# Half products of 21 `up` pairs on an x2 that is not yet normalised

## The chip, the core and the metric

One core of a Trainium2 chip runs the whole kernel, one hybrid decoder layer on 512 tokens of width 1024. The metric is the device time of one execution in microseconds (us). The time before is the median of 3 runs.

Engines are named as the profile names them: PE is TensorE (matmuls; PEld its weight loads), DVE is VectorE, ACT is ScalarE, POOL is GpSimd, SP is SyncE. SP issues the plain DMAs, GpSimd those that add to what lies at their destination (`accum_op`, here called accumulates).

## The reference

Only the last part of the layer is changed. `x` after the attention part is called x2 in the kernel.

```python
def rms_norm(x, g):
    xf = x.astype(jnp.float32)
    y = xf * lax.rsqrt(jnp.mean(xf * xf, axis=-1, keepdims=True) + RMS_EPS)
    return (y * g.astype(jnp.float32)).astype(x.dtype)
...
        x = x + (gate_pool * y_pool + gate_nsa * y_nsa) @ w_out[l]
        h = rms_norm(x, ffn_norm_g[l])
        gate_pre, val = jnp.split(h @ w_up[l], 2, axis=-1)
        gate_c = causal_dwconv(gate_pre, conv_w[l], conv_b[l])
        x = x + (jax.nn.silu(gate_c) * val) @ w_down[l]
```

`D_MODEL` is 1024, `D_FF` 2816, `CONV_WIDTH` 3 and `DEPTH` 1. The norm's factor is one number per token; the gain `g` is one number per feature.

## The kernel before

**Layout and precision.** Activations lie transposed: 128 features on the partitions, 512 tokens along the free axis, so x2 is 8 tiles of 128 x 512. Each float32 operand a of a product is split into a high part and a low part in the matmul's rounded float32 type, and a product is three matmuls: high by high, high by low, low by high. `split` makes the high part on ACT and the low one on DVE; `split_by_dma` writes -x on ACT into the low tile, rounds x into the high tile on ACT, and has a GpSimd DMA add x to the low tile. Weights are loaded as raw tiles of 128 x 1024 into rings of three (`wraw`, and `whi`, `wlo` for their parts).

**Order.** No instruction is issued where the code stands. `Plan` records every operation with what it reads and writes, then plays the whole list through with its own costs, gives each operation a due time, and writes out an order for each engine (line 395 issues all of them, so every row of the profile has line 395). TensorE keeps the order of recording (in the attention part it merges two such streams); DVE, ACT, POOL and SP are ordered by due time. The engines run these orders strictly; semaphores do the rest. Small working tiles come from a pool of 54 pages of 128 x 512.

**Stages.** After the attention part come the products with `w_nsa_out` (lines 1081 to 1102), then `out` (lines 1107 to 1124): for f in 0, 4, 1, 5, 2, 6, 3, 7, 24 matmuls of 512 columns give one tile of x2; it is added to x, multiplied by the gain and split into gh and gl, and its square goes into `acc`. `norm_rstd` (line 556) sums `acc` over the features by 8 small matmuls and takes the inverse root on DVE in twelve small steps; `bcast_rstd` (line 565) spreads the result over the partitions as `rb` by way of four diagonal tiles and 8 matmuls.

**`up`, `w_up` in 22 pairs.** Pair f is 128 columns of gate_pre and the same 128 of val. `up_plain` (line 1173), for f = 0 to 3, multiplies gh, gl by both weight tiles, 24 matmuls of 512 columns each, and multiplies by `rb` behind PSUM. In pair 0 the norm's matmul stands behind the gate's 24 matmuls, and the broadcast behind the first 15 of val's.

`up_fast` (line 1260), for f = 4 to 21, sees a pair as a 2 x 2 product of halves: the features in two halves of 4 tiles, the tokens in two halves of 256 columns, the two weight tiles as the other side. With seven half products instead of eight (and sums of halves on either side) it gets the same four results. A half product (`product`, line 1199) is 4 x 3 matmuls of 256 columns. The sums of the weights' halves (`s3`, `h1` to `h5`) are made on DVE from the raw halves `rg`, `r1`, `r2`, and four of the five are split with an accumulate. The loads of r1 and r2 wait for the first product of the pair two before (`begun[-2]`, line 1263). The sums of x2's halves are made once, in `halves` (line 1140), on x2 already multiplied by the gain and by `rb`; that is why it stands behind pair 0. It gives nh and nl (x2's halves themselves) and th and tl (their sums).

Three PSUM banks serve a pair: bx, by and bq. The first product goes to bx and is copied to by, on which the second goes on; two results on the way are read off by ACT (u2 and u3, the halves of `u1`) and added by DVE to what bq holds. Two of the seven products are put off into the next pair (`held`: `end1`, `end2`), and with them the pair's `conv` (a bias and three taps, then Silu) and the split of y = silu x val.

**`down`.** y's first 16 tiles go into x2 in four groups of four, each group 8 products of 12 matmuls of 512 columns, called fills here (`dn_group`, line 1227). `AT` says before which pair a group is ready, and `FILL` how many fills stand where: one number ahead of the pair, and three inside it. The first group starts with `both`, which takes two banks. y's last 6 tiles are multiplied at the very end (lines 1341 to 1360).

**The start.** Eight matmuls of a tile of ones (line 495) run while the first loads are under way.

Of the kernel before, what the change touches and what calls it, by code (L numbers as in the profile page):

```python
# [15 lines left out]
P = 128  # L16
# [3 lines left out]
KD = 8  # L20
# [32 lines left out]
PLAIN = 4  # L53
DIRECT = (0, 3)
AT = (4, 9, 13, 17)
FILL = {f: (0, 0, 0, 0) for f in range(22)}
FILL.update({4: (0, 4, 0, 0), 5: (0, 1, 0, 0), 6: (0, 1, 0, 0), 7: (0, 1, 0, 0), 8: (0, 1, 0, 0)})
FILL.update({f: (0, 1, 1, 0) for f in range(9, 18)})
# [340 lines left out]
def hybrid_layer(ctx: ExitStack, tc: tile.TileContext, xT, pos, par, cst, poolw, w1, wa, wb, wf,  # L399
# [95 lines left out]
    for i in range(8):  # L495
        PE.matmul(pt[:, 0:P], ones, ones, start=(i == 0), stop=(i == 7))
# [59 lines left out]
    def norm_rstd(acc_tile, dst, tag):  # L556
        pt = bank(tag)
# [19 lines left out]
    for k in range(KD):  # L577
# [6 lines left out]
        if k == 6:  # L584
            for j in range(KD):
                square_x(j)
            norm_rstd(acc, rstd, "mm")
            DVE.tensor_scalar_mul(rhalf, rstd, 0.5)
# [515 lines left out]
    x2, gh, gl = [None] * KD, [None] * KD, [None] * KD  # L1104
    acc = page("acc")
    ffng = R("ffng")
    for f in (0, 4, 1, 5, 2, 6, 3, 7):
# [6 lines left out]
        tail = pl.last()  # L1114
        x2[f] = pl.tile(sb, (P, T), F32, "x2", "pp", 10)
        DVE.tensor_add(x2[f], pt, xres)
        gh[f], gl[f] = page("gh", dt=F32R), page("gl", dt=F32R)
        split(gh[f], gl[f], x2[f], ffng[:, f:f + 1])
        if f:
            sq = page("sq")  # L1120
            ACT.activation(sq, x2[f], AF.Square)
            DVE.tensor_add(acc, acc, sq)
        else:
            ACT.activation(acc, x2[f], AF.Square)

    rstd2 = keep("rstd", (P, NT))
    convb = R("convb")
    nh, nl, th, tl = {}, {}, {}, {}
    yh, yl = [None] * KF, [None] * KF
    tt = pl.tile(sb, (P, 4, T), F32R, "th", "ptc", 1)  # L1130
    t2 = pl.tile(sb, (P, 3, T), F32R, "th", "t_cst", 1)
    t3 = [pl.tile(sb, (P, T), F32R, n, "t_" + n, 1) for n in ("oraw", "ot")]
    b11 = [[pl.tile(sb, (P, T), F32R, "nh", "pt", 6) for _ in range(2)] for _ in range(2)]

    def split_by_dma(hi, lo, x):
        ACT.activation(lo, x, AF.Copy, scale=-1.0)
        POOL.dma_start(lo, x, accum_op=ALU.add)
        ACT.activation(hi, x, AF.Copy)

    def halves(k):  # L1140
        u = [page("xb"), page("xb")]
        for x, j in zip(u, (k, k + 4)):
            DVE.scalar_tensor_tensor(x, x2[j], ffng[:, j:j + 1], rb, op0=ALU.mult, op1=ALU.mult)
        c = slice((k % 2) * H2, (k % 2 + 1) * H2)
        nh[k], nl[k] = (b11[k // 2][i][:, c] for i in range(2))
        split(nh[k], nl[k], u[0][:, :H2])
        nh[k + 4] = pl.tile(sb, (P, T), F32R, "nh", "pt", 6) if k < 2 else page("nh", dt=F32R)
        nl[k + 4] = pl.tile(sb, (P, T), F32R, "nl", "pp", 10) if k < 2 else page("nl", dt=F32R)
        split_by_dma(nh[k + 4], nl[k + 4], u[1])
        b1, b2 = u[0], u[1]  # L1150
        ta, tb = page("ta"), page("tb")
        DVE.tensor_sub(ta[:, :H2], b1[:, :H2], b1[:, H2:])
        DVE.scalar_tensor_tensor(ta[:, H2:], ta[:, :H2], -1.0, b2[:, H2:], op0=ALU.mult, op1=ALU.subtract)
        DVE.tensor_sub(tb[:, :H2], b2[:, H2:], b1[:, H2:])
        DVE.scalar_tensor_tensor(tb[:, H2:], ta[:, H2:], -1.0, b2[:, :H2], op0=ALU.mult, op1=ALU.subtract)
        for i, x in ((0, ta), (1, tb)):
            th[k, i] = tt[:, k] if i == 0 else t2[:, k] if k < 3 else t3[0]
            tl[k, i] = page("tl", dt=F32R) if k or i else t3[1]
            (split_by_dma if i else split)(th[k, i], tl[k, i], x)

# [12 lines left out]
    def up_plain(f):  # L1173
        pts = []
        for s in range(2):
# [9 lines left out]
            if f == 0 and s == 0:  # L1185
                norm_rstd(acc, rstd2, "tr")
# [269 lines left out]
```

## Time and profile before

| | |
|---|---|
| median of 3 runs | 693.01 us (692.36 to 693.43) |
| the profiled execution | 693.21 us |
| its span, first to last instruction | 691.4 us |
| matmul records | 4060 |
| DMA packets | 45703, 113.99 MB |

How to read the rows that follow: a group's row gives engine, operation, the tiles written and read by the program's names (buffer numbers left out), the shape, the number of instructions, then their busy time and the mean ns of one, then the engine's idle time before them and what ended it. The wait view names who was waited for, the time in all, how often, and the longest. The chain of waits follows the work that ended last back to the start, and is listed in order of time: start, length, what. The timeline lists start and length of each instruction. Spans of matmuls overlap, since they are pipelined; the spacing of two starts is what one costs.

### The profile page before, as it was taken

Reading aid. Unit: us, or ns where it says so; the run is one execution under the profiler, and the core shown is the slowest. Engines: PE = TensorE matmul, PEld = TensorE weight load, DVE = VectorE, ACT = ScalarE, POOL = GpSimd, SP = SyncE. Lnnn points to the kernel's source line nnn. Section 1 sums busy time; section 2 is a strip of 40 time slices with the busy share of each in tenths; the row PEclk is TensorE's granted clock in tenths of the full one; section 3 lists DMA queues with packets and bytes.
Section 4 is the critical chain, followed back from the end, with each engine's and each line's share of the span. In section 5 each row is a group of like instructions: output and inputs, shape, how many; then the busy total and the mean of one; then the engine's idle time right before and its main releaser. Section 6 shows DMA issues by size and latency. Waiting matters only on the chain.

```text
span 691.4 us, 11144 instructions
## 1 busy us (share of the span) xinstructions
PE 687.2 (99%) x4060; PEld 606.8 (88%) x4060; DVE 479.6 (69%) x1032; ACT 432.2 (63%) x795; POOL 98.3 (14%) x124
## 2 busy tenths in 40 slices
PE   9999999999999999999999999999999999999998
PEld 8898978888888888888888899999999999999987
DVE  6768568878787644765569967777776766675542
ACT  7667677776777653334459758778677656674320
POOL 0011100000000000000022223223222112220000
PEclk9999999999999999999999999999999999999999
DMA  8468534655556557844379778779888866764131
GB/s 299 143 164 248 139 105 92 155 137 138 152 122 151 154 137 229 278 152 144 125 159 255 173 176 210 171 168 225 203 198 189 205 155 159 179 168 101 46 129 62
DMA packets 45703, 113.99 MB, mean 165 GB/s; under 512 B 5328, under 2 KB 6096, under 8 KB 45648
## 3 DMA queue, kind: packets, MB, share of 16 engines
q1 hardware_dynamic: 29520, 76.43, 34.3%
q0 software_dynamic: 15840, 36.71, 29.5%
q8 instruction: 32, 0.52, 0.3%
q14 instruction: 23, 0.19, 0.1%
q10 hardware_dynamic: 288, 0.14, 0.1%
HBM read 70.27 MB, written 6.29 MB: 111 GB/s over the span
## 4 chain that ended last, share of the span: by engine, by line
PE 99%; DMA 0%; ACT 0%; DVE 0%; SPq 0%; issue 0%; ACTq 0%
PE mm L395 42%; PE tr L395 32%; PE sc L395 14%; PE av L395 11%; DMA xr<-xT 0%; ACT xh L395 0%; DVE o L395 0%; SPq L395 0%; ACTq L395 0%
## 5 line engine op out<-in xcount | busy, mean ns | idle before, releaser
L395 ACT ACTIVATE whi<-wraw 128x1024 fp32r<-128x1024 f32 (+2 forms) x96 | 97.1, 1013 | 70.4 <-issue 29.0
L395 DVE TENSOR_TENSOR wlo<-wraw,whi 128x1024 fp32r<-128x1024 f32 (+1 forms) x66 | 76.3, 1158 | 15.6 <-ACT whi L395 14.6
L395 POOL DMA_DIRECT2D wlo<-wraw x30 | 25.9, 865 | 331.6 <-ACT wlo L395 273.9
L395 PE MATMUL mm<-xh,whi 128*128 128x512 f32 x176 | 73.0, 415 | 0.0
L395 PE MATMUL mm<-xh,wlo 128*128 128x512 f32 x176 | 69.1, 393 | 0.0
L395 PE MATMUL mm<-xl,whi 128*128 128x512 f32 x176 | 68.9, 391 | 0.0
L395 PE MATMUL mm<-tl,sh 128*128 128x256 f32 x190 | 53.5, 282 | 0.0
L395 PE MATMUL mm<-th,sl 128*128 128x256 f32 x174 | 49.1, 282 | 0.0
L395 PE MATMUL mm<-th,sh 128*128 128x256 f32 x174 | 49.0, 281 | 0.0
L395 ACT ACTIVATE wlo<-wraw 128x1024 fp32r<-128x1024 f32 x30 | 31.7, 1060 | 21.6 <-PE mm L395 13.6
L395 POOL DMA_DIRECT2D sl<-r x36 | 31.0, 860 | 87.0 <-ACT sl L395 64.6
L395 PE MATMUL sc<-yh,whi 128*128 128x512 f32 x104 | 40.5, 389 | 0.0
L395 PE MATMUL sc<-yl,whi 128*128 128x512 f32 x104 | 40.5, 389 | 0.0
L395 PE MATMUL sc<-yh,wlo 128*128 128x512 f32 x104 | 40.5, 389 | 0.0
L395 PEld LDWEIGHTS mm<-xh,wlo 128*128 128x128 f32 x176 | 33.0, 188 | 7.5
L395 DVE SCALAR_TENSOR_TENSOR ft<-fg,pr,ft 128x511 f32<-128x511 f32 (+1 forms) x44 | 32.9, 749 | 9.6 <-ACT ft L395 8.9
L395 ACT ACTIVATE pp<-pp,asm 128x384 f32<-128x384 f32 (+3 forms) x64 | 35.4, 557 | 5.8 <-DVE asm L395 5.8
L395 PEld LDWEIGHTS mm<-xh,whi 128*128 128x128 f32 x176 | 33.2, 188 | 4.6
L395 PEld LDWEIGHTS mm<-xl,whi 128*128 128x128 f32 x176 | 33.3, 189 | 4.2
L395 PEld LDWEIGHTS mm<-tl,sh 128*128 128x128 f32 x190 | 35.7, 188 | 0.4
L395 PEld LDWEIGHTS mm<-th,sh 128*128 128x128 f32 x174 | 32.7, 188 | 1.0
L395 PEld LDWEIGHTS mm<-th,sl 128*128 128x128 f32 x174 | 32.7, 188 | 0.0
(399 smaller groups left out, 2078.9 us busy)
## 6 DMA issues: line engine op xcount, KB each, us to landing
wlo<-wraw POOLq DMA_DIRECT2D x30, 512.0 KB, 4.5
wraw<-wup SPq DMA_DIRECT2D x26, 512.0 KB, 4.0
wraw<-wf SPq DMA_DIRECT2D x22, 512.0 KB, 3.6
r<-wup SPq DMA_DIRECT2D x36, 256.0 KB, 5.0
sl<-r POOLq DMA_DIRECT2D x36, 256.0 KB, 5.4
wraw<-wdn SPq DMA_DIRECT2D x16, 512.0 KB, 4.1
sl<-s POOLq DMA_DIRECT2D x18, 256.0 KB, 5.9
sl<-wraw POOLq DMA_DIRECT2D x18, 256.0 KB, 4.7
```

The costliest lines, as they stand in the source:

```text
L395: getattr(self.real[o.eng], method)(*a, **kw)
```

## The change

- `PLAIN` is now (0,): pairs 1, 2 and 3 are taken by `up_fast` too, so 21 of 22 pairs use half products. `AT` begins at 5 instead of 4, and pairs 1 to 4 have no fill; pairs 5 to 17 have two each, 18 to 21 one each. `both` is gone.
- The sums of x2's halves are made by `sums(k)` inside `out`, as soon as x2[k] and x2[k + 4] are there, on x2 times the gain. `halves`, nh and nl are gone; gh and gl take their places, and are kept for all pairs.
- What comes out of PSUM in `up_fast` is multiplied by `rb`: two copies become multiplications by `rb` on DVE (one of the two was on ACT), and two sums get a multiplication behind them.
- The third product of the first pair by half products, which has none put off from before it, stands second.
- r1 and r2 of pairs 1 and 2 wait for groups of `out`, since `begun` now begins with these.
- The norm's matmul takes another PSUM bank, and nine matmuls of ones run at the start instead of eight.

```diff
 NCST = _o
 PAGES = 54
 RINGS = {"wraw": 3, "whi": 3, "wlo": 3}
-PLAIN = 4
-DIRECT = (0, 3)
-AT = (4, 9, 13, 17)
+PLAIN = (0,)
+DIRECT = (0,)
+AT = (5, 9, 13, 17)
 FILL = {f: (0, 0, 0, 0) for f in range(22)}
-FILL.update({4: (0, 4, 0, 0), 5: (0, 1, 0, 0), 6: (0, 1, 0, 0), 7: (0, 1, 0, 0), 8: (0, 1, 0, 0)})
-FILL.update({f: (0, 1, 1, 0) for f in range(9, 18)})
+FILL.update({f: (0, 1, 1, 0) for f in range(5, 18)})
 FILL.update({18: (0, 1, 0, 0), 19: (0, 1, 0, 0), 20: (0, 1, 0, 0), 21: (0, 1, 0, 0)})
 TRIES = 12
 RESERVE = 3
...
     POOL.memset(ones, 1.0)
     ACT.dma_start(pr[:, 0:16], par[:, 0:16])
     pt = bank("mm")
-    for i in range(8):
-        PE.matmul(pt[:, 0:P], ones, ones, start=(i == 0), stop=(i == 7))
+    for i in range(9):
+        PE.matmul(pt[:, 0:P], ones, ones, start=(i == 0), stop=(i == 8))
     xr, xh, xl = [None] * KD, [None] * KD, [None] * KD
     acc = page("acc")
...
     rb = keep("rb", (P, T))
-    def norm_rstd(acc_tile, dst, tag):
-        pt = bank(tag)
+    def norm_rstd(acc_tile, dst, pt):
         with pl.unit():
             for t in range(NT):
                 PE.matmul(pt[:, t:t + 1], acc_tile[:, t * P:(t + 1) * P], ones[:, 0:1], start=True, stop=True)
...
             if f > 1:
                 tail = nots[f - 2]
-    x2, gh, gl = [None] * KD, [None] * KD, [None] * KD
+    x2, gh, gl, begun = [None] * KD, [None] * KD, [None] * KD, []
     acc = page("acc")
     ffng = R("ffng")
+    less = keep("less", (P, KD))
+    DVE.tensor_scalar_mul(less, ffng, -1.0)
+    th, tl = {}, {}
+    tt = pl.tile(sb, (P, 4, T), F32R, "th", "ptc", 1)
+    t2 = pl.tile(sb, (P, 3, T), F32R, "th", "t_cst", 1)
+    t3 = [pl.tile(sb, (P, T), F32R, n, "t_" + n, 1) for n in ("oraw", "ot")]
+
+    def split_by_dma(hi, lo, x):
+        ACT.activation(lo, x, AF.Copy, scale=-1.0)
+        POOL.dma_start(lo, x, accum_op=ALU.add)
+        ACT.activation(hi, x, AF.Copy)
+
+    def sums(k):
+        a, b = x2[k], x2[k + 4]
+        ta, tb, b2 = page("ta"), page("tb"), page("b2")[:, :H2]
+        ACT.activation(b2, b[:, H2:], AF.Copy, scale=ffng[:, k + 4:k + 5])
+        DVE.tensor_sub(tb[:, H2:], a[:, :H2], a[:, H2:])
+        ACT.activation(ta[:, :H2], tb[:, H2:], AF.Copy, scale=ffng[:, k:k + 1])
+        DVE.scalar_tensor_tensor(tb[:, :H2], a[:, H2:], less[:, k:k + 1], b2, op0=ALU.mult, op1=ALU.add)
+        DVE.scalar_tensor_tensor(ta[:, H2:], ta[:, :H2], -1.0, b2, op0=ALU.mult, op1=ALU.subtract)
+        DVE.scalar_tensor_tensor(tb[:, H2:], b[:, :H2], less[:, k + 4:k + 5], ta[:, H2:], op0=ALU.mult, op1=ALU.subtract)
+        for i, x in ((0, ta), (1, tb)):
+            th[k, i] = tt[:, k] if i == 0 else t2[:, k] if k < 3 else t3[0]
+            tl[k, i] = page("tl", dt=F32R) if k or i else t3[1]
+            (split_by_dma if i else split)(th[k, i], tl[k, i], x)
+
     for f in (0, 4, 1, 5, 2, 6, 3, 7):
         xres = page("xres")
         with pl.behind(tail):
...
         pt = any_bank()
         mm3(pt, wh, wl, mh, ml, 0, KD)
         tail = pl.last()
+        begun.append(tail)
         x2[f] = pl.tile(sb, (P, T), F32, "x2", "pp", 10)
         DVE.tensor_add(x2[f], pt, xres)
-        gh[f], gl[f] = page("gh", dt=F32R), page("gl", dt=F32R)
+        for q in (gh, gl):
+            home = ("pt", 6) if f in (0, 4, 1) else ("pp", 10) if f == 5 else ("pg", PAGES)
+            q[f] = pl.tile(sb, (P, T), F32R, "gh", home[0], home[1])
         split(gh[f], gl[f], x2[f], ffng[:, f:f + 1])
         if f:
             sq = page("sq")
...
             DVE.tensor_add(acc, acc, sq)
         else:
             ACT.activation(acc, x2[f], AF.Square)
+        if f > 3:
+            sums(f - 4)
     rstd2 = keep("rstd", (P, NT))
     convb = R("convb")
-    nh, nl, th, tl = {}, {}, {}, {}
     yh, yl = [None] * KF, [None] * KF
-    tt = pl.tile(sb, (P, 4, T), F32R, "th", "ptc", 1)
-    t2 = pl.tile(sb, (P, 3, T), F32R, "th", "t_cst", 1)
-    t3 = [pl.tile(sb, (P, T), F32R, n, "t_" + n, 1) for n in ("oraw", "ot")]
-    b11 = [[pl.tile(sb, (P, T), F32R, "nh", "pt", 6) for _ in range(2)] for _ in range(2)]
-
-    def split_by_dma(hi, lo, x):
-        ACT.activation(lo, x, AF.Copy, scale=-1.0)
-        POOL.dma_start(lo, x, accum_op=ALU.add)
-        ACT.activation(hi, x, AF.Copy)
-
-    def halves(k):
-        u = [page("xb"), page("xb")]
-        for x, j in zip(u, (k, k + 4)):
-            DVE.scalar_tensor_tensor(x, x2[j], ffng[:, j:j + 1], rb, op0=ALU.mult, op1=ALU.mult)
-        c = slice((k % 2) * H2, (k % 2 + 1) * H2)
-        nh[k], nl[k] = (b11[k // 2][i][:, c] for i in range(2))
-        split(nh[k], nl[k], u[0][:, :H2])
-        nh[k + 4] = pl.tile(sb, (P, T), F32R, "nh", "pt", 6) if k < 2 else page("nh", dt=F32R)
-        nl[k + 4] = pl.tile(sb, (P, T), F32R, "nl", "pp", 10) if k < 2 else page("nl", dt=F32R)
-        split_by_dma(nh[k + 4], nl[k + 4], u[1])
-        b1, b2 = u[0], u[1]
-        ta, tb = page("ta"), page("tb")
-        DVE.tensor_sub(ta[:, :H2], b1[:, :H2], b1[:, H2:])
-        DVE.scalar_tensor_tensor(ta[:, H2:], ta[:, :H2], -1.0, b2[:, H2:], op0=ALU.mult, op1=ALU.subtract)
-        DVE.tensor_sub(tb[:, :H2], b2[:, H2:], b1[:, H2:])
-        DVE.scalar_tensor_tensor(tb[:, H2:], ta[:, H2:], -1.0, b2[:, :H2], op0=ALU.mult, op1=ALU.subtract)
-        for i, x in ((0, ta), (1, tb)):
-            th[k, i] = tt[:, k] if i == 0 else t2[:, k] if k < 3 else t3[0]
-            tl[k, i] = page("tl", dt=F32R) if k or i else t3[1]
-            (split_by_dma if i else split)(th[k, i], tl[k, i], x)
-
     def conv(f, g, pg):
         t = page("ft")
         ACT.activation(t, pg, AF.Identity, scale=convw[:, f, 2:3], bias=convb[:, f:f + 1])
...
             if s == 0:
                 begun.append(pl.last())
             if f == 0 and s == 0:
-                norm_rstd(acc, rstd2, "tr")
+                norm_rstd(acc, rstd2, bank("sc", (P, 2, T))[:, 0])
         pg, pv = pts
         y, g = page("y"), page("fg")
         DVE.tensor_mul(g, pg, rb)
...
     def mov(i, half):
         if i == 0:
-            return (lambda k: nh[k]), (lambda k: nl[k])
+            return tuple((lambda k, q=q: q[k][:, :H2]) for q in (gh, gl))
         if i == 1:
-            return tuple((lambda k, q=q: q[k + 4][:, half * H2:(half + 1) * H2]) for q in (nh, nl))
+            return tuple((lambda k, q=q: q[k + 4][:, half * H2:(half + 1) * H2]) for q in (gh, gl))
         return tuple((lambda k, q=q: q[k, i - 2][:, half * H2:(half + 1) * H2]) for q in (th, tl))
-    held, begun, fills = [], [], []
+    held, fills = [], []
     def finish():
         while held:
...
             part(pt, c, a, 0, 4)
             DVE.tensor_add(x2[2 * c + a], pt, x2[2 * c + a])
-        def both(free):
-            load(0)
-            pts = any_bank(), any_bank()
-            for k0, k1 in ((0, 3), (3, 4)):
-                for a in range(2):
-                    part(pts[a], 0, a, k0, k1)
-            for a in range(2):
-                DVE.tensor_add(x2[a], pts[a], x2[a])
-
-        if g == 0:
-            fills.extend((both, lambda free: None))
-        for c in range(g == 0, 4):
+        for c in range(4):
             for a in range(2):
                 fills.append(lambda free, c=c, a=a: one(c, a, free))
     def up_fast(f, n1, n2, n3):
         rg, r1, r2 = ring("wraw"), soon("r1"), soon("r2")
         SP.dma_start(rg, flat(wup[f, 0]))
-        with pl.behind(begun[-2]):
+        with pl.behind(begun[-2 - max(0, 3 - f)]):
             SP.dma_start(r1, flat(wup[f, 1, :, 0:4]))
             SP.dma_start(r2, flat(wup[f, 1, :, 4:8]))
...
         del held[:]
         if more:
             more[0]()
-        fill(n1, f == PLAIN)
+        else:
+            product(bq, h1, mov(2, 0), True)
+        fill(n1)
         product(by, h2, mov(2, 1), False)
         ACT.activation(u2, by[:, :H2], AF.Copy)
         if more:
             more[1]()
         fill(n3)
-        product(bq, h1, mov(2, 0), True)
+        if more:
+            product(bq, h1, mov(2, 0), True)
         product(bx, halves_(a1, 1), mov(1, 0), False)
-        ACT.activation(g[:, :H2], bx[:, :H2], AF.Copy)
+        DVE.tensor_mul(g[:, :H2], bx[:, :H2], rb[:, :H2])
         fill(n2)
         product(by, h3, mov(3, 0), False)
         ACT.activation(u3, by[:, :H2], AF.Copy)
         DVE.tensor_add(y[:, H2:], bq[:, :H2], u3)
+        DVE.tensor_mul(y[:, H2:], y[:, H2:], rb[:, H2:])
         def end1():
             product(by, h5, mov(3, 1), False)
-            DVE.tensor_copy(y[:, :H2], by[:, :H2])
+            DVE.tensor_mul(y[:, :H2], by[:, :H2], rb[:, :H2])
         def end2():
             product(bq, h4, mov(1, 1), False)
             DVE.tensor_add(g[:, H2:], bq[:, :H2], u2)
+            DVE.tensor_mul(g[:, H2:], g[:, H2:], rb[:, H2:])
             t = conv(f, g, g)
             DVE.scalar_tensor_tensor(y, y, -1.0, t, op0=ALU.mult, op1=ALU.mult)
             split_y(f, y)
...
         if f in AT:
             dn_group(AT.index(f))
         fill(FILL[f][0], True)
-        if f < PLAIN:
+        if f in PLAIN:
             up_plain(f)
         else:
             up_fast(f, *FILL[f][1:])
-        if f == 0:
-            for k in range(4):
-                halves(k)
     fill(1, True)
     finish()
     fill(9, True)
```

More of the change, by code (lines that the diff above doesn't have):

```diff
@@ L586, in hybrid_layer @@
                 square_x(j)
-            norm_rstd(acc, rstd, "mm")
+            norm_rstd(acc, rstd, bank("mm"))
             DVE.tensor_scalar_mul(rhalf, rstd, 0.5)
```

## The prediction

> **What bounds the kernel now.** I read the page first, then TensorE's waits, then the chain of waits.
>
> ```profile
> span 691.4 us, 11144 instructions
> PE 687.2 (99%) x4060; PEld 606.8 (88%) x4060; DVE 479.6 (69%) x1032; ACT 432.2 (63%) x795; POOL 98.3 (14%) x124
> PE 99%; DMA 0%; ACT 0%; DVE 0%; SPq 0%; issue 0%; ACTq 0%
> PE mm L395 <- POOL ones L395: 1.0, 1, 1.0
> ```
>
> The fourth line is the whole view of who made TensorE wait: one wait, at the very start. The chain that ended last (third line) is TensorE in 99% of the span. So the time is the number of matmuls times their spacing, and an edit counts only if it changes that number, or makes an operand late. The spacing comes from the chain in order of time, where each row gives the time from its first matmul to the next row's:
>
> ```profile
> 344.10 5.44 PE av L395 x24
> 349.54 0.79 PE tr L395 x8
> 350.32 3.57 PE mm L395 x15
> 356.84 10.88 PE tr L395 x48
> 413.02 2.84 PE mm L395 x24
> ```
>
> A 512-column matmul takes 5.44/24 = 0.2267 us, a 256-column one 2.84/24 = 0.1183 us. A plain pair is 48 of the first, 10.88 us (pair 1 is the fourth row). A pair by half products is 7 products of 12 of the second, 1.42 us each, 9.94 us together. The difference is 0.94 us a pair.
>
> **The change, part by part.** *Three more pairs by half products (f = 1, 2, 3).* The instruction lists of the two built kernels show 144 fewer 512-column matmuls and 252 more 256-column ones: -144 x 0.2267 + 252 x 0.1183 = -32.64 + 29.82 = **-2.82 us**, all on the path. The row norm's matmuls (the 0.79 us row, and the broadcast behind 15 matmuls of `val`) stay where they were; another PSUM bank for the first costs nothing.
>
> *Nine warming matmuls.*
>
> ```profile
> 0.99 3.78 PE L395 MATMUL mm<-ones 128*128 128x128 f32 x16 [0.99 <-POOL ones L395]
> 4.27 0.91 ACT L395 ACTIVATE xh<-xr,pr 128x256 fp32r<-128x256 f32 x2 [1.12 <-DMA xr<-xT]
> 4.83 1.65 PE L395 MATMUL tr<-whi,xh 128*128 128x512 f32 x3
> 6.28 0.52 PE L395 MATMUL av<-whi,xh 128*128 128x512 f32 x1
> 6.64 0.63 PE L395 MATMUL sc<-whi,xh 128*128 128x256 f32 x4
> ```
>
> Eight (two records each) last 3.78 us, about 0.43 each, and end at 4.77; the first real matmul starts at 4.83. The ninth pushes it back by 0.17 us (if the next may start before the last record ends, as in the pipelined rows) to 0.4. The first four real matmuls take 6.64 - 4.83 = 1.81 us, 0.45 each, twice 0.2267: the clock is still low. If it rises at the same instant, the delay costs half of itself, 0.1 to 0.2 us. At the other end, if the unbroken stream lets it rise before 4.83, up to 1.81 - 4 x 0.2267 = 0.9 us is won. I take +0.1, since no row shows an earlier rise. The Trainium skill ("TensorE: Matmul & The Clock Gate", Part 1) says that the warm-up is a budget of time in a free-running window, not a number of matmuls; by it the term is the delay alone, +0.1 to +0.2, and the rise may fall elsewhere in each execution.
>
> *The half sums move into `out`*, on x2 times the gain, and `halves` (with its eight products with `rb`) goes.
>
> ```profile
> 300.40:343.90 43.50, 43.50 (x193) 36.04 (x192) 24.99 (x32) 17.05 (x23) 0.00 (x0) 1.00 0.44 141
> 363.00:397.00 34.00, 34.00 (x157) 28.40 (x156) 32.27 (x55) 28.25 (x46) 8.64 (x10) 1.00 0.89 213
> 412.90:463.80 50.90, 50.90 (x388) 49.03 (x387) 38.42 (x59) 37.98 (x70) 13.78 (x16) 1.00 0.81 187
> 494.00:616.00 122.00, 122.00 (x867) 114.92 (x866) 84.73 (x129) 81.40 (x145) 28.27 (x33) 1.00 0.77 176
> ```
>
> These are windows: length, then busy time of TensorE, weight loads, VectorE, ScalarE, GpSimd, then clock, DMA share, GB/s. The first is `out`: VectorE 25.0 of 43.5 us, ScalarE 17.1. Four `sums` add on VectorE four 256-column operations and a split, about 4 x 0.42 + 0.69 = 2.4 us each, 9.5 us; on ScalarE about 2.6 each, 10.5. With the first weights of pair 1 that is some 38 and 31 of 43.5: covered. Without that cover it would be up to 9.5 us. What is queued behind them on VectorE is the x2 of the last group and the norm's twelve small operations; these must follow the norm's matmul at once, because its diagonal stops TensorE 15 matmuls later. Walking that queue, I find 0.2 to 0.9 us to spare.
>
> *The row norm behind PSUM.* Each pair now multiplies four 256-column halves by `rb` on VectorE: two of these replace a copy (one ScalarE's, one its own), two are new.
>
> ```profile
> L395 DVE TENSOR_TENSOR wlo<-wraw,whi 128x1024 fp32r<-128x1024 f32 x36 | 44.0, 1222 | 12.2 <-ACT whi L395 12.1
> L395 DVE SCALAR_TENSOR_TENSOR ft<-fg,pr,ft 128x511 f32<-128x511 f32 x22 | 16.5, 749 | 8.9 <-ACT ft L395 8.9
> L395 DVE TENSOR_TENSOR yl<-y,yh 128x512 fp32r<-128x512 f32 x22 | 15.1, 684 | 2.5 <-ACT yh L395 2.5
> L395 DVE TENSOR_TENSOR sl<-wraw,sh 128x512 fp32r<-128x512 f32 x18 | 12.4, 688 | 6.5 <-ACT sh L395 6.3
> L395 DVE SCALAR_TENSOR_TENSOR y<-y,ft 128x512 f32<-128x512 f32 x18 | 12.3, 685 | 1.4 <-ACT ft L395 1.2
> L395 DVE TENSOR_TENSOR s<-wraw,r 128x512 f32<-128x512 f32 x18 | 12.3, 682 | 0.9 <-DMA r<-wup 0.9
> L395 DVE COPY y<-mm 128x256 f32<-128x256 f32 x17 | 7.2, 423 | 8.0 <-PE mm L395 8.0
> L395 DVE TENSOR_TENSOR y<-tr,u 128x256 f32<-128x256 f32 x17 | 7.1, 418 | 0.1
> 413.05 0.69 DVE L395 TENSOR_TENSOR x<-sc,x 128x512 f32<-128x512 f32 x1 [1.16 <-PE sc L395]
> 413.66 0.68 DVE L395 TENSOR_TENSOR s<-wraw,r 128x512 f32<-128x512 f32 x1
> L395 ACT ACTIVATE whi<-wraw 128x1024 fp32r<-128x1024 f32 x38 | 40.1, 1055 | 14.2 <-PE av L395 6.1 <-PE sc L395 5.1 <-issue 1.8
> L395 ACT ACTIVATE sl<-r 128x512 fp32r<-128x512 f32 x36 | 22.4, 621 | 1.6 <-DMA r<-wup 1.6
> L395 ACT ACTIVATE u<-mm 128x256 f32<-128x256 f32 x34 | 13.0, 383 | 31.1 <-PE mm L395 25.1 <-issue 5.3
> 414.80 0.62 ACT L395 ACTIVATE sl<-r 128x512 fp32r<-128x512 f32 x1
> 415.32 0.62 ACT L395 ACTIVATE sh<-r 128x512 fp32r<-128x512 f32 x1
> ```
>
> VectorE per pair: 1.22 (a1's low part) + 4 x 0.685 (adds) + 0.69 + 2 x 0.75 + 0.685 + 0.68 + six of 0.42 = **10.0 us**. Before, every such pair had one or two fills of `down` (12 x 0.2267 = 2.72 us of TensorE); now pairs 1 to 4 have none, and offer 9.94 us. But the two timeline rows show the next operation starting 0.61 us after one that lasts 0.69, so back to back it is nearer 9.5. ScalarE has 1.06 + 9 x 0.62 + 3 x 0.38 + three of 0.62 to 0.81, 9.8 us by durations, but its rows start 0.52 apart, so about 8.2: covered. VectorE's weights run ahead: in the built order the low part of pair f's `a1` stands a whole pair before its use, and h2's about 3 us before. Four pairs at 0.1 us short eat 0.4 of these 3. I take +0.1 here; the upper end is the second rival.
>
> *Loads and accumulating DMAs of the unfilled pairs.*
>
> ```profile
> q1 hardware_dynamic: 29520, 76.43, 34.3%
> r<-wup SPq DMA_DIRECT2D x36, 256.0 KB, 5.0
> sl<-r POOLq DMA_DIRECT2D x36, 256.0 KB, 5.4
> ```
>
> A pair loads 1 MB and issues four accumulates of 256 KB. The third window is four pairs with one fill (1.25 MB loaded): 0.81 x 12.72 = 10.3 us of DMA time a pair; the fourth has two fills (1.5 MB, 15.4 us): 0.77 x 15.4 = 11.9. By that slope an unfilled pair needs 8.75 us; by the queue's mean (34.3% of 691.4 us for 76.4 MB, 3.1 us/MB) 10.3 - 0.8 = 9.5; out of 9.94. Closest use: pair 3's h1. Its raw halves are released by pair 1's first product (the `behind` at line 1263) and land 5 us later; VectorE has them summed about 11.1 us after pair 1's start, ScalarE cast at 15.2, the accumulate lands at 20.6, and TensorE takes it at 7.1 + 9.94 + 4 x 1.42 = 22.7: 2 us to spare. What queues behind a late one is GpSimd's next three accumulates, then the products that use them. The first fill of pair 5 is as close: `down`'s low part and y of pair 3, 0 to 1 us. For such seams I take +0.2 (bounds 0 and 2.7, next).
>
> **Sum:** -2.82 + 0.1 + 0.1 + 0.2 = **-2.4 us**. The profiled execution took 693.21 us (span 691.4 and 1.8 around it), so 690.8; the median of the runs is 0.2 lower, so **690.6 us**.
>
> **The rivals.** (1) *Late operands at a seam*: the norm's diagonal, pair 5's first fill, or an h1 that lands 7.5 to 8.5 us after its issue instead of 5.4. For: spare times under 2 us. Against: before, no operand was late after 1 us. Two such at 0.5 to 1.3 us cost 1 to 2.7: about 692.0 us.
>
> (2) *VectorE becomes the bound of pairs 1 to 4.* Its busiest stretch (second window) is 32.27/34 = 95%. At that it needs 10.0/0.95 = 10.6 us a pair, 0.6 short, 2.5 over four pairs: the 3 us of lead just hold; with half of it gone, 1 us is lost: 691.7. The Trainium skill ("VectorE: DVE Perf Modes", "The DRAIN you can't avoid") says that the next operation waits until the pipe has emptied. By that rule the durations add up whole, 4 x 0.1 = 0.4 us, without lead 691.0; the 0.61 us spacing disagrees.
>
> (3) *The DMA engines become the bound*, and the kernel is **slower**. The highest share above is 0.89; at 0.81, that of pairs 5 to 8, an unfilled pair needs 10.8 to 11.7 us, so 0.9 to 1.8 late, 3.5 to 7 over four pairs, less 2 of spare: up to +5. The time would be 692 to 695.6, at the upper half 694.8. It decides from a pair of 9.94 + 2.82/4 = 10.65 us, plus the spare. For: the low windows already show 0.8 to 0.9 busy. Against: an unfilled pair moves 2 MB in 9.94 us, 201 GB/s, and the second window held 213 for 34 us with TensorE never waiting.
>
> (4) *The clock rises early*: 0.9 won, 689.6. (5) *The change doesn't do what it says*, the half products cost as much as plain ones: 693. The counts above and equal forms already at 0.1183 speak against it.
>
> **Chances.** Forecast 0.52, rival 1 0.2, 2 0.08, 3 0.1, 4 0.06, 5 0.04. About 0.2% (1.4 us) can be told from no change here: faster means under 691.6, slower over 694.4. Faster: 0.52 + 0.06 + 0.06 of rival 1 + 0.04 of rival 2 + 0.01 of rival 3 = 0.69; slower 0.06 of rival 3 and 0.02 for what I have not seen, 0.08; same 0.23. The range, from rival 4 to the upper end of rivals 1 and 2, is 689.5 to 692.8; above it is most of rival 3.
>
> **What would show it.** Right: the waits of TensorE keep one line, the counts are 144 and 252 off, pairs 1 to 4 take 9.94 us each in the chain, and the first full-speed matmul comes within 0.2 us of 6.64. Wrong: rows of TensorE waiting for DVE `diag`, ACT `u` or a DMA `sl<-r` between the end of `out` and pair 6 (rivals 1 and 3, told apart by the DMA share there), or VectorE above 95% in that stretch with `sl<-wraw` as releaser (rival 2).

## The result, and the profile after

The change made the kernel slower. After it the median is 698.63 us (695.90 to 701.65, 6 runs), before it 692.47 us on the same chip (691.79 to 693.43, 6 runs): ratio 1.0079, 95% interval 1.0067 to 1.0092. The medians lie 6.2 us apart; by the ratio it is 5.5. The forecast was 690.6, and the range ended at 692.8. The profiled execution took 696.96 us, one of the shorter ones, so the stalls below are those of a mild case.

The page of the changed kernel, its first two lines and the chain of waits by engine, then the whole view of who made TensorE wait:

```profile
span 695.2 us, 11505 instructions
PE 686.5 (99%) x4170; PEld 609.6 (88%) x4170; DVE 502.8 (72%) x1103; ACT 436.9 (63%) x802; POOL 101.9 (15%) x128
...
PE 82%; DMA 11%; ACT 3%; DVE 3%; issue 2%; SPq 0%; POOL 0%; POOLq 0%; ACTq 0%; DVEq 0%
```

```profile
PE tr L394 <- ACT u L394: 2.5, 4, 1.2
PE mm L394 <- POOL ones L394: 1.0, 1, 1.0
PE sc L394 <- DVE yl L394: 0.8, 1, 0.8
PE mm L394 <- DMA sl<-r: 0.6, 1, 0.6
PE mm L394 <- DVE yl L394: 0.2, 1, 0.2
```

TensorE still counts as 99% busy, because a waiting stretch of 1 us is small against 695. But DMA, ScalarE and VectorE, 0% of the chain before, now hold 17% of it, and one wait has become eight. For the size I add up, over all matmuls of 128 x 256 and 128 x 512, the time to the next start beyond 0.1183 or 0.2267 us ("excess"), by stretches of the span (in us from its start). The kernel before has less than 0.05 us in each stretch.

| excess, us | 357-400 | 400-465 | 465-620 | 620-end | all |
|---|---|---|---|---|---|
| after | 2.25 | 1.85 | 2.23 | 0.81 | 7.1 |

The balance closes: the last matmul ends at 691.73 us instead of 688.28, 3.45 later; the counts changed by -144 and +252 as planned, worth -2.82, the excess is +7.1, and 0.8 us were won in the first microseconds, where the clock happened to rise early (last section).

There are three kinds of stall, and one single one. *First, h1 in the unfilled pairs.* GpSimd's queue, then the DMA issues of 357 to 400 us with their median time from issue to landing:

```profile
371.55 0.86 POOL L394 DMA_DIRECT2D sl<-r  x1 [0.18 <-issue]
```

```profile
sl<-r POOLq DMA_DIRECT2D x8, 256.0 KB, 7.1
r<-wup SPq DMA_DIRECT2D x8, 256.0 KB, 7.3
```

The accumulate of pair 3's h1 is issued at 371.55 us, 0.3 us behind the prediction's walk (15.2 us after pair 1's start at 356.05), but it lands at 379.5, after 7.9 us, not 5.4. TensorE was there at 378.7 and stood for 0.75 us. The DMA engines are 0.90 busy in this stretch (first row of the windows below), and both kinds of transfer take 7 us.

The single one is the larger stall of this stretch: 1.1 us at 398.8, where the first fill of pair 5 waits for pair 3's `yl` (third row of the waits above, 0.8 us). VectorE makes `yl` only at 399.40, since its order has a weight's low part in front, and that weight's load landed at 397.15. The prediction had named this seam, with 0 to 1 us to spare.

*Second, loads of r1 and r2 that come too late in the later pairs.* The chain of waits in order of time, and ScalarE's timeline at the same place:

```profile
435.94 1.35 PE tr L394 x12
437.29 5.82 DMA r<-wup
...
443.13 0.63 ACT sl L394
443.76 0.28 ACT u L394
```

```profile
439.89 1.06 ACT L394 ACTIVATE whi<-wraw 128x1024 fp32r<-128x1024 f32 x1
443.13 0.63 ACT L394 ACTIVATE sl<-r 128x512 fp32r<-128x512 f32 x1 [2.18 <-DMA r<-wup]
443.67 0.37 ACT L394 ACTIVATE u<-tr 128x256 f32<-128x256 f32 x1
```

Read from below: TensorE waits for `u`, a copy out of PSUM whose product had ended at about 442.9. The copy stood in ScalarE's queue behind a cast of r, which had waited 2.18 us for its load; and the load was issued only at 437.29. Why so late? SP's waits between 415 and 616 us, and its timeline at one pair:

```profile
SPq L394 <- DMA sl<-r: 64.1, 10, 10.1
SPq L394 <- DMA sl<-wraw: 55.1, 14, 7.2
```

```profile
536.50 0.33 SPq L394 DMA_DIRECT2D wraw<-wup  x1
542.15 0.80 SPq L394 DMA_DIRECT2D r<-wup  x2
```

SP issues the pair's first load and then stands for over 5 us before r1 and r2. It waits for `sl<-r`, an accumulate of an earlier pair: not for data, but for the buffer ("page") that the accumulate still reads or writes. r1, r2, their sums and the parts of h1 to h5 all live in 54 such pages.

*Third, the tail.* The chain behind the last product of pair 21:

```profile
653.97 1.43 PE mm L394 x12
...
655.43 0.44 DVE fg L394
...
655.89 0.44 DVE fg L394
...
659.34 0.86 DVE wlo L394
660.20 0.61 DVE y L394
...
661.50 0.70 DVE yl L394
...
662.24 0.73 PE mm L394 x2
```

From the product to the split of y it takes 6.8 us (655.4 to 662.2); the fill and the first products of the last stage that stand there keep TensorE busy to 661.7. Two things make this longer than before. The second `fg` row is one of the new multiplications by `rb`. And `wlo`, a weight's low part that y does not need, stands in front of y in VectorE's order, where the kernel before has it behind:

```profile
656.42 0.69 DVE L395 SCALAR_TENSOR_TENSOR y<-y,ft 128x512 f32<-128x512 f32 x1 [0.16 <-ACT ft L395]
657.15 0.96 DVE L395 TENSOR_TENSOR wlo<-wraw,whi 128x768 fp32r<-128x768 f32 x1
```

By the starts of VectorE's operations in the two timelines, the way from `fg` to the end of `yl` grew by 0.8 us (5.96 to 6.76): 0.4 up to the convolution's taps, where the new multiplication stands, 0.6 from there to y, where `wlo` now stands, less 0.2 behind y.

Last, windows (columns as in the prediction) for comparison with experiments:

```profile
357.00:400.00 43.00, 41.72 (x338) 40.46 (x337) 34.74 (x59) 34.91 (x64) 12.93 (x15) 1.00 0.90 200
400.00:465.00 65.00, 63.69 (x443) 59.47 (x444) 51.34 (x86) 44.85 (x79) 17.54 (x21) 1.00 0.82 189
465.00:620.00 155.00, 153.63 (x1085) 144.10 (x1084) 116.19 (x191) 99.05 (x171) 35.08 (x41) 1.00 0.71 170
```

### The profile page after: what moved, and what is told of

It is laid out like the page before. It is cut to its first block, busy times and chain, and to the rows that moved or that the text cites. A ratio compares the mean times of both kernels' runs of the same rounds, so it can differ in the third digit from the quotient of the medians.

```text
span 695.2 us, 11505 instructions
## 1 busy us (share of the span) xinstructions
PE 686.5 (99%) x4170; PEld 609.6 (88%) x4170; DVE 502.8 (72%) x1103; ACT 436.9 (63%) x802; POOL 101.9 (15%) x128
## 4 chain that ended last, share of the span: by engine, by line
PE 82%; DMA 11%; ACT 3%; DVE 3%; issue 2%; SPq 0%; POOL 0%; POOLq 0%; ACTq 0%; DVEq 0%
PE mm L394 35%; PE tr L394 26%; PE sc L394 11%; PE av L394 10%; DMA r<-wup 6%; DMA sl<-r 4%; ACT sl L394 1%; ACT whi L394 1%; DMA wraw<-wup 1%; ACT sh L394 1%; DVE wlo L394 1%; DVE ft L394 0%; ACT ft L394 0%; SPq L394 0%; DVE yl L394 0%
## 5 line engine op out<-in xcount | busy, mean ns | idle before, releaser
L394 PE MATMUL tr<-gh,whi 128*128 128x256 f32 x336 | 61.6, 281 | 0.0
L394 POOL DMA_DIRECT2D sl<-r x42 | 36.2, 862 | 134.2 <-ACT sl L394 61.9
L394 PEld LDWEIGHTS tr<-gh,whi 128*128 128x128 f32 x336 | 51.6, 188 | 0.1
L394 PE MATMUL sc<-yl,whi 128*128 128x512 f32 x120 | 46.8, 390 | 0.8 <-DVE yl L394 0.8
L394 PE MATMUL tr<-gh,wlo 128*128 128x256 f32 x168 | 47.3, 282 | 0.0
L394 PE MATMUL sc<-yh,whi 128*128 128x512 f32 x120 | 46.9, 391 | 0.0
L394 PE MATMUL sc<-yh,wlo 128*128 128x512 f32 x120 | 46.7, 389 | 0.0
L394 ACT ACTIVATE sl<-r 128x512 fp32r<-128x512 f32 x42 | 26.2, 623 | 21.0 <-DMA r<-wup 19.3
L394 PE MATMUL tr<-tl,sh 128*128 128x256 f32 x121 | 34.1, 282 | 0.0
L394 PE MATMUL tr<-th,sh 128*128 128x256 f32 x110 | 31.4, 286 | 2.5 <-ACT u L394 2.5
```

The lines of the kernel that those rows point to most:

```text
L394: getattr(self.real[o.eng], method)(*a, **kw)
```

## The experiments

The theory from these rows was that pages are short. Before the change, nh and nl of k = 0 to 3 were stored as halves, two to a buffer; the products by halves use only the first 256 columns of gh and gl there, yet the changed kernel keeps them whole, and so holds four pages more to the end. The rivals: the DMA engines are too full in pairs 1 to 4 and all else is backlog; or VectorE is, with its extra multiplications. Every edit lets the recording layer plan the order of all engines anew, so the times of two variants can differ by more than their edit, and one profile is one execution.

### Four pages given back, and taken away again

```diff
+    def pack():
+        for k in (2, 3):
+            ACT.activation(gh[k - 2][:, H2:], f32(gh[k][:, :H2]), AF.Copy)
+            DVE.tensor_copy(gl[k - 2][:, H2:], f32(gl[k][:, :H2]))
+        packed.append(1)
...
             up_fast(f, *FILL[f][1:])
+        if f == 1:
+            pack()
```

From pair 2 on, `mov(0, ...)` reads k = 2, 3 from the second halves of k = 0, 1.

> The changed kernel, but once pair 1 is through, the used halves of gh and gl of k = 2, 3 are copied into the dead second halves of k = 0, 1 (four copies of 256 columns, two on ScalarE, two on VectorE), so that four of the 54 pages come free. Page theory (loads of r1 and r2 wait for pages, because gh and gl hold four pages more than nh and nl did): the excess over pairs 5 to 18 (1.9 us between 400 and 465 us and 2.2 us between 465 and 620 us of the changed kernel's profile) goes, the 2.2 us before 400 us stays: about 694.5 us. DMA theory (transfers of the unfilled pairs 1 to 4 are too many, and what comes later is their backlog): nothing changes, 698.6 us, within 1. VectorE theory (the multiplications with rb fill VectorE's queue): nothing changes either, or 0.4 us more.

Measured: 692.55 us (10 runs) against 693.12 of before on that chip, ratio 0.9993 (0.9984 to 1.0002). About 6 us are gone, more than the 4 expected from the mild profile. Windows of this kernel, the first of SP's waits between 415 and 616 us, and SP's timeline at a pair:

```profile
357.00:400.00 43.00, 42.30 (x344) 41.44 (x343) 38.27 (x65) 36.47 (x67) 13.76 (x16) 1.00 0.87 194
400.00:465.00 65.00, 65.00 (x462) 61.23 (x461) 51.72 (x84) 44.48 (x79) 17.23 (x20) 1.00 0.89 205
465.00:620.00 155.00, 155.00 (x1103) 146.12 (x1102) 119.02 (x195) 104.19 (x179) 36.96 (x43) 1.00 0.75 177
```

```profile
SPq L394 <- DMA sl<-wraw: 98.5, 15, 10.6
```

```profile
531.25 0.33 SPq L394 DMA_DIRECT2D wraw<-wup  x1
531.68 0.85 SPq L394 DMA_DIRECT2D r<-wup  x2
```

Behind 400 us TensorE is busy without a gap, though the DMA engines do more there (0.89 instead of 0.82) and VectorE too. `sl<-r` is gone from SP's large waits (0.9 us are left of 64.1), and here r1 and r2 follow the first load at once.

An edit can gain by a luckier order. So the copies stayed and the pages were taken away (`PAGES = 50`):

> Pack with 50 pages instead of 54: the four copies stay, the four pages that they free are taken away again. Page theory: the loads of r1 and r2 are late again and the time comes back to that of the changed kernel, 697 to 700 us, with waits of TensorE for ACT u behind 400 us. If pack gained by something else (another planned order, which each edit makes anew): 692.5 us, within 1.

Measured: 696.47 us (696.17 to 699.88, 5 runs), ratio 1.0054 (1.0039 to 1.0069): 4.2 of the 6 us come back by the ratios, a little less than expected. The profiled execution was the slowest of the five, 699.88 us, so its stalls are those of a severe case. SP's waits and the windows of this kernel:

```profile
SPq L394 <- DMA sl<-r: 63.3, 10, 10.5
```

```profile
400.00:465.00 65.00, 62.93 (x436) 58.33 (x435) 51.23 (x84) 44.12 (x78) 17.22 (x20) 1.00 0.83 191
465.00:620.00 155.00, 152.32 (x1071) 142.70 (x1071) 115.35 (x192) 97.91 (x170) 34.39 (x40) 1.00 0.73 170
```

The same wait comes back with the same size, and so do the stalls. In the changed kernel the second kind of stall hangs on the four pages, and not on the copies or on a luckier order. Whether too few pages are enough by themselves is another question.

### Fewer pages before; three pairs plain again

The same in the kernel before, with `PAGES = 50`:

> The kernel before with 50 pages instead of 54, nothing else. Page theory: it becomes slower by some 2 to 4 us, 694.5 to 696.5 us, and TensorE now waits for ACT u in the half-product pairs, behind loads of r that are issued late. DMA theory and VectorE theory: 692.5 us, one wait of TensorE as before.

Measured: 693.37 us (10 runs), ratio 1.0008 (0.9999 to 1.0017); TensorE keeps its one wait. Here the page theory fails as it was put: 50 pages less the four that nh and nl took leave as many as the changed kernel has, yet its profile has 0.2 us of excess, and by the interval it costs 1.2 us at most. And the changed kernel with three pairs plain:

```diff
-PLAIN = (0,)
-DIRECT = (0,)
+PLAIN = (0, 1, 2, 3)
+DIRECT = (0, 3)
```

> The changed kernel with pairs 1 to 3 as plain products again (weights of pairs 0 and 3 split on VectorE as before the change), all else of the change kept: half sums in out, rb behind PSUM, nine warming matmuls, the plan of fills. The matmuls gain back 2.82 us. DMA theory: no stall is left, and the earlier clock rise (0.8 us) stays: 691.7 us. Page theory: the stalls from pair 4 on stay, 3 to 4 us: 695 us. VectorE theory: with 0.84 us more of VectorE a pair the stalls of the later pairs stay too: 694 to 695 us.

Measured: 695.02 us (6 runs), ratio 1.0032 (1.0021 to 1.0043). That is the 695 us of the page theory, but not for its reason: it expected stalls of 3 to 4 us from pair 4 on, and the excess of the profile is 0.0 before 465 us, 0.49 up to 620 and 0.88 in the tail, 1.4 in all, beside a time 1.9 above before. So the number was luck. Short pages without the three pairs thus have 0.2 (before with 50 pages) and 0.5 us of excess between 400 and 620 us, the three pairs without short pages 0.1 (pack), and both together 4.1. It takes both. Who waits for the loads of r hints at how they go together; the changed kernel's ScalarE and VectorE between 400 and 616 us:

```profile
ACT sl L394 <- DMA r<-wup: 18.2, 11, 3.9
DVE s L394 <- DMA r<-wup: 12.6, 8, 4.4
DVE r L394 <- DMA r<-wup: 3.6, 4, 1.0
```

These three add up to 34 us. The same sum is 30 in pack with 50 pages, 14 in pack and 14 in the kernel before with 50 pages, 0 with pairs 1 to 3 plain, and 1 in the kernel before. So 14 us of such waits still cost TensorE next to nothing, and 30 or more do not stay hidden. My reading is that the unfilled pairs use up the lead of the loads, and that with pages short the loads cannot win it back; no run measured that lead by itself.

### What is left in pairs 2 to 4

Pack's profile still has 1.27 us of excess before 400 us, two waits for h1's accumulate. Two ways to take them away: split h1 on VectorE,

```diff
-        h1 = summed(r1)
+        if f in (2, 3, 4):
+            h1 = pair()
+            split(*h1, r1)
+        else:
+            h1 = summed(r1)
```

> Pack, with h1 of pairs 2 to 4 split on ScalarE and VectorE instead of by an accumulating DMA (three transfers of 256 KB fewer, 0.69 us more of VectorE in each of these pairs). Bandwidth theory and order theory: the waits for sl<-r at 379 and 390 us go, about 1 us less, 691.5 us. VectorE theory (VectorE is the bound of these pairs: 38.3 of 43 us there already): the 2.1 us come back as waits for DVE, 693 us or more.

or take other transfers out of its way. This second kernel leaves out the accumulates of h3, h4 and h5 in pairs 2 to 4, so their low parts are not the right ones; it serves to measure the landing of what is left.

```diff
+            if f in (2, 3, 4) and x is not r1:
+                ACT.activation(lo, x, AF.Copy, scale=-1.0)
+                ACT.activation(hi, x, AF.Copy)
+            else:
+                split_by_dma(hi, lo, x)
```

> Pack, with the accumulating DMAs of h5, h3 and h4 in pairs 2 to 4 left out (the low parts there hold minus the high ones only), h1's kept. Nine transfers of 256 KB less. Bandwidth theory: h1's accumulate, 6.9 us at the median between 357 and 400 us in pack, lands in 4 to 5 us, loads of r in 4 instead of 6.6, and TensorE waits for none: 691.5 us. If a landing of 7 us is how long such a transfer takes beside loads whatever else is queued: 6 to 7 us still.

Measured: the first 691.49 us (10 runs), ratio 0.9976 (0.9967 to 0.9986); excess 0.01 before 400 us. VectorE, the third theory, is a little busier there than in pack (38.9 us instead of 38.3; the kernel before had 40.2) and holds nothing up, as this window shows:

```profile
357.00:400.00 43.00, 43.00 (x355) 42.53 (x354) 38.88 (x66) 34.02 (x62) 10.49 (x13) 1.00 0.82 188
```

The second 692.34 us (8 runs), not the 691.5 expected: its stretch has no excess either, but its plan has a new stall of 1.15 us at 426, again behind `u`, so its time says little of the transfers. The landing times answer the question. DMA issues between 357 and 400 us, pack first, then this kernel:

```profile
sl<-r POOLq DMA_DIRECT2D x8, 256.0 KB, 6.9
r<-wup SPq DMA_DIRECT2D x8, 256.0 KB, 6.6
```

```profile
r<-wup SPq DMA_DIRECT2D x8, 256.0 KB, 4.2
...
sl<-r POOLq DMA_DIRECT2D x6, 256.0 KB, 5.0
```

Nine accumulates fewer (DMA share 0.61 instead of 0.87), and a load of r lands in 4.2 us, an accumulate in 5.0. So what a landing takes beyond 4 to 5 us is contention between the transfers of these pairs. The DMA share alone does not show it: in the kernel before it was 0.86 in this stretch, and an accumulate `sl<-r` landed in 4.1 us, a load of r in 5.9 (medians of 3 and 4).

### The order of the loads

```diff
+        s4 = soon("s4")
-        DVE.tensor_add(rg[:, 512:], rg[:, 512:], rg[:, :512])
-        h4 = summed(rg[:, 512:])
+        DVE.tensor_add(s4, rg[:, 512:], rg[:, :512])
+        h4 = summed(s4)
```

> The kernel with the four copies (pack), and the sum that becomes h4 goes to a page of its own instead of the second half of the pair's raw ring buffer: the next loads into that ring then wait for the sum, not for the landing of h4's accumulating DMA. Order theory (between 357 and 400 us the loads come late because SP's queue waits for that landing, 44.9 us of SP's waits there, and loads and accumulates then start in one burst): the two waits of TensorE for DMA sl<-r (0.56 and 0.47 us in the profile of pack) go, the share of the DMA engines there falls little: 691.4 us, 1.1 less than pack. Bandwidth theory (the engines are full there, 0.87 to 0.90): the same bytes, the same waits: 692.5 us.

Measured: 704.63 us (4 runs), ratio 1.0164, the worst of all, which no theory had. SP's two largest waits between 415 and 616 us:

```profile
SPq L394 <- DVE wlo L394: 96.2, 13, 8.3
SPq L394 <- DVE s L394: 89.7, 14, 11.7
```

Buffers made by `soon` are handed their pages in one fixed line, in the order of the code. With s4 in that line, the next pair's loads can have a page only after VectorE has come to s4's sum; the loads then wait for a computation that was meant to run behind them. With `page("s4")`, outside the line, and on top of the edits of the next section:

> The same as with the three edits, and the sum that becomes h4 goes to a page of its own, which now isn't in the fixed line in which loads and splits are handed their pages (in the first form of this edit SP waited 90 us for DVE s behind 415 us, because the loads stood behind that sum in the line). Order theory: SP no longer waits for the landing of h4's accumulate, all loads come earlier; but no wait of TensorE is left to be won: 690.0 us, as without it. Page theory: one page more per pair is short again, and waits for ACT u or ACT sh come back: 691 to 695 us.

Measured: 696.28 us (4 runs), ratio 1.0046 (1.0030 to 1.0062), above every expectation. SP now waits 43.8 us for DVE `sl`, and TensorE for ACT `sh`. Giving s4 a page of its own cost more than it won in either form; by which way the second loses was not followed further, and whether another order of the loads would help with enough pages stays open.

### The tail, the warming matmul, and all together

```diff
-FILL.update({18: (0, 1, 0, 0), 19: (0, 1, 0, 0), 20: (0, 1, 0, 0), 21: (0, 1, 0, 0)})
+FILL.update({18: (0, 1, 0, 0), 19: (0, 1, 0, 0), 20: (0, 1, 0, 0), 21: (0, 0, 0, 0)})
```

> Pack, and the one fill of down in pair 21 is moved behind that pair's last two products, so that two fills stand there. Tail theory (the sum and the multiplication with rb stand one behind the other in front of the last convolution, and TensorE waits for the last y at 657 us): 0.8 us less, 691.7 us, and the excess after 620 us falls from 0.81 to below 0.2. If the excess comes from elsewhere: 692.5 us.

Measured: 691.35 us (8 runs), ratio 0.9980 (0.9970 to 0.9990); the tail's excess falls from 0.81 to 0.00. Two things changed, though: the last product now has a second fill of 2.7 us behind it, and in the new plan y stands in front of `wlo` again (653.04 and 655.64 us), which shortens the way from `fg` to `yl` from 6.76 to 6.15. Every profile with this stall has `wlo` in front of y, and every one without it has not. How much of the 0.8 us is the multiplication by `rb` and how much the order rests on the rows shown with the tail; neither was changed by itself.

The kernel before with nine warming matmuls:

> The kernel before with nine warming matmuls instead of eight, nothing else. If the ninth is what lets the clock rise before the first real matmul (4.74 us in the changed kernel's profile, 6.54 before), it gains 0.8 us: 691.7 us. If the rise moves from execution to execution, whatever the number, or costs what the ninth takes: 692.5 us, within 0.3.

Measured: 692.93 us (11 runs), ratio 0.9997 (0.9988 to 1.0006): nothing. Then the three edits on one kernel, with nine and with eight:

> Pack, the fill of pair 21 moved behind the last two products, and h1 of pairs 2 to 4 split on VectorE, together. If the three losses are separate (pages 400 to 620 us, landing of h1 at 379 and 390 us, tail at 657 us), no wait of TensorE is left behind 1 us and the 2.82 us of fewer matmuls are all that counts: 690.0 us, 2.8 below before. If they stand in for one another (one wait gone, the next comes): 691.3 us, as each alone.

> The same with eight warming matmuls instead of nine; every other instruction stands where it stood. If the ninth costs what it takes: 0.2 us less. If it makes the clock rise earlier: up to 0.8 us more. If the rise moves by itself between executions (3.9 to 7.0 us in the profiles with nine so far, 6.5 and 7.2 with eight): within 0.3 of the other.

Measured: 690.63 us (690.05 to 690.91) with nine and 690.51 (690.34 to 690.69) with eight, 5 runs each, against 692.92 of before: ratios 0.9968 (0.9955 to 0.9980) and 0.9967 (0.9955 to 0.9980). Both kernels are faster than before and than the changed one. The ninth matmul is worth nothing that shows. The page of the kernel with eight:

```profile
span 688.6 us, 11458 instructions
...
PE 99%; DMA 0%; ACT 0%; DVE 0%; SPq 0%; issue 0%; ACTq 0%
```

| excess, us | 357-400 | 400-465 | 465-620 | 620-end | ratio to before |
|---|---|---|---|---|---|
| after | 2.25 | 1.85 | 2.23 | 0.81 | 1.0079 |
| pack, 50 pages | 1.24 | 2.91 | 3.60 | 0.83 | 1.0054 |
| pairs 1 to 3 plain | 0.00 | 0.01 | 0.49 | 0.88 | 1.0032 |
| pack | 1.27 | 0.06 | 0.02 | 0.81 | 0.9993 |
| pack, tail | 1.99 | 0.01 | 0.03 | 0.00 | 0.9980 |
| pack, h1 on VectorE | 0.01 | 0.01 | 0.03 | 0.85 | 0.9976 |
| all three, nine | 0.01 | 0.58 | 0.02 | 0.00 | 0.9968 |
| all three, eight | 0.01 | 0.01 | 0.02 | 0.00 | 0.9967 |

The 1.99 of the tail's kernel before 400 us, where pack has 1.27, stands in a stretch that this edit does not touch: so much a new plan or another execution can move.

## Why the prediction was wrong

*Three more pairs, -2.82.* Right. In the profile of the kernel with all three edits and eight warming matmuls, which has no excess behind 357 us, the last matmul ends at 685.16 us instead of 688.28; 0.26 of these 3.1 us were won in the first 52 us, and 2.86 are left. That its runs are 2.3 to 2.4 us faster than before, as the prediction's sum had it, is luck as far as the three small terms go: they were not what the runs found, and the interval of the ratio (1.4 to 3.1 us) does not tell -2.4 from -2.82.

*Late operands at seams, +0.2 (bounds 0 and 2.7).* This is the step that failed: with what the tail cost, the runs show 8 us in its place (by the ratios 6.0 for the late loads, 1.2 for h1, 0.9 for the tail). The walk looked at loads, casts and accumulates of pairs 1 to 5 with the durations of the old kernel, and at no buffer. What it left out is that gh and gl, put in the place of nh and nl, hold four pages more for the whole rest of the kernel, so that, with three more unfilled pairs ahead of them, r1 and r2 are issued late in the pairs behind too. By the ratios of after and pack that is 0.86%, 6 us; in the profiles 4.0 of the 5.0 us of excess that pack takes away lie behind 400 us, most of it where the prediction had no term and no rival: behind pair 6. That the pages are held longer can be read from the code, and SP's queue is the place to look: in the profile of before its waits could have been split into those for data and those for a buffer.

*h1 of the unfilled pairs.* The walk was right up to the issue; the landing was mis-sized, 7.9 us instead of 5.4, against a spare of 2. It had its place in rival 1 (an h1 that lands after 7.5 to 8.5 us) at 1 to 2.7 us; measured 1.2, by the ratios of pack with and without the split on VectorE. The other seam it had named, pair 5's first fill, came up 1.1 us short in the changed kernel; in pack, with `yl` at 396.3 us, it did not wait.

*DMA engines, rival 3.* Its sign and its time (692 to 695.6) came nearest, and the share did reach 0.90 at transfers of 7 us. But the engines were not the bound of a pair: with the pages back the kernel moved as many bytes and lost 1.3 us in this stretch. Its chance of 0.1 was too low all the same, because the argument against it ("213 GB/s with TensorE never waiting") came from a stretch of plain pairs, whose operands lie further ahead.

*VectorE, +0.1 and rival 2.* VectorE was no bound, and its demand was sized a little high: 38.9 of 43 us in the kernel with h1 on VectorE, 9.0 us in 9.94 where the prediction had 9.5 to 10.0, with no excess at all. But the two new multiplications were priced in pairs 1 to 4 alone. At the end of pair 21 one of them stands in a chain with one fill for cover, and that tail cost 0.8 to 0.9 us, of which the chain's rows give it some 0.4 and VectorE's order the rest; the prediction had it at nothing and named no cover.

*The half sums in `out`, and the norm's diagonal.* Right: no excess in the changed kernel between 300 and 345 us, and 0.24 between 345 and 357 us in either kernel.

*The ninth matmul, +0.1 (bounds -0.9 and +0.4).* Nothing measurable, for the reason in the last section.

## What to carry to other kernels

An operand that lives longer is a buffer that is missing elsewhere: count the buffers that an edit adds or frees, then ask which load waits for one, and what stands in the queues behind that load. The shortage cost 0.2 to 0.5 us of stalls where the first pairs were plain, and 6 us where three more pairs went by half products; test two such parts singly and together. And price an added instruction once more at the last iteration, where little comes after it to cover it, and look there at what else stands in its engine's order.

## What the runs showed of the hardware

*When the clock rises is chance.* TensorE's first rows of the changed kernel, as against 4.83 to 6.48 for the first three real matmuls of before:

```profile
0.99 4.04 PE L394 MATMUL mm<-ones 128*128 128x128 f32 x18 [0.99 <-POOL ones L394]
4.79 0.93 PE L394 MATMUL tr<-whi,xh 128*128 128x512 f32 x3
```

The ninth warming matmul took no time from the real ones (they start at 4.79, before at 4.83). By the traces' records of the clock it reached full speed between 3.9 and 7.2 us in fourteen profiles, at 3.9, 6.5 and 7.2 us in the three with eight matmuls and from 3.9 to 7.1 with nine. The first real matmuls run at half speed until then, so one execution may start up to about 1.2 us faster than another of the same kernel ((7.2 - 4.8)/2, an estimate from these rows).

*A stall can cost more than its length.* The first kernel with s4 in windows of the records' own limits:

```profile
378.00:382.20 4.20, 1.99 (x15) 1.57 (x14) 3.59 (x9) 3.46 (x8) 2.41 (x3) 1.00 0.74 124
382.30:385.60 3.30, 3.30 (x18) 3.30 (x17) 0.57 (x1) 1.54 (x3) 0.86 (x1) 0.50 1.00 220
385.70:389.00 3.30, 3.30 (x30) 3.30 (x29) 1.88 (x4) 0.93 (x2) 0.00 (x0) 1.00 0.83 212
```

After a stretch in which TensorE was busy 1.99 of 4.2 us, the granted clock is 0.50 for 3.41 us, and 18 matmuls run where 30 run next. The same happened at 395.9 us there, and at 368.7 us in the second kernel with s4. The rise at 6.80 us and the fall at 382.27 lie 110 times 3.4133 us apart. The Trainium skill ("TensorE: Matmul & The Clock Gate", Part 1) has a free-running window of 3413 ns; the records agree. The Trainium skill, in the same page's section "HAM oscillation — how this bites in real kernels", puts the danger at idle gaps of more than about 3.4 us; here no single wait of TensorE was longer than 2.0 us, and one such with shorter ones in the same window was enough. Counted in windows of 3.4133 us from the rise on, TensorE was busy 0.35, 0.47 and 0.42 of the window just before the three falls. In all other such windows of the fourteen profiles up to 685 us it was busy 0.54 or more (0.54 in pack with 50 pages, the window that ends at 416.7 us; 0.66 at the least in the changed kernel), and the clock stayed up.
